# A third K-tile pair by Strassen's scheme in the FFN inputs, and sums of weights begun by an accumulating DMA

## The chip, the core and the metric

The kernel runs on one core of a Trainium2 chip. The core has a matrix engine (TensorE, PE in the profile; its weight loads are listed as PEld), a vector engine (VectorE, DVE), a scalar engine (ScalarE, ACT), a general engine (GpSimd, POOL) and a queue processor (SyncE, SP) that here only issues transfers. Each engine works through its own instruction list in order and waits at an instruction until what it needs is there. Transfers (DMAs) are issued from the lists of SP, ACT or POOL and then run on 16 shared DMA engines. The metric is the device time of one execution in microseconds (us).

## The reference

One layer of a streaming encoder on 256 tokens of width 2048, all in float32: a gated FFN, a mixer of two attentions, a cross attention to 256 memory tokens, and a second gated FFN, each followed by a residual and a layer norm. The change touches the two FFNs:

```python
D_MODEL, SEQ, D_FF = 2048, 256, 5504
def swiglu_ffn(x, w_in, w_out):
    g, u = jnp.split(x @ w_in, 2, axis=-1)
    return (jax.nn.silu(g) * u) @ w_out
...
h = layer_norm(ALPHA * h + 0.5 * swiglu_ffn(h, ffn1_w_in[l], ffn1_w_out[l]), ln_ffn1_g[l], ln_ffn1_b[l])
...
h = layer_norm(ALPHA * h + 0.5 * swiglu_ffn(h, ffn2_w_in[l], ffn2_w_out[l]), ln_ffn2_g[l], ln_ffn2_b[l])
```

All weights are read once from HBM; for each FFN `w_in` is 2048 x 11008 and `w_out` 5504 x 2048.

## The kernel before

**Numbers.** Every float32 operand is split into a rounded high part and the rest (`split`, lines 242 to 244): ScalarE casts the high part, VectorE subtracts it from the source. A product is then three passes on TensorE: high times high, low times high, high times low.

**Weights.** `run` (line 160) walks over a list of work items, each with the weights that it needs. A weight is a tile of 128 partitions by 2048 floats (1 MB), loaded by a transfer in SP's list into one of three buffers called `raw` (`fetch`, line 171). `load` (line 190) then splits it into two units of 1024 columns, each a pair of tiles `hi` and `lo`; there are four units. An item's weight is prepared at most one item ahead, since two units belong to the running item and two to the next (`ahead`, line 222). A planner arranges the instructions of each engine once, when the program is built: it takes those that are ready in an order of priority, which is the order of the code, shifted for work that is marked `SOON` or `LATE`. On the chip that order is fixed.

**FFN input.** The output columns go in groups of 512 gate and 512 up columns. A group's four results (two halves of 128 tokens, gate and up) lie in four PSUM banks, and its eight weights cover the 16 K tiles in pairs: c = 0 to 7 (`pair_group`, line 572). A plain pair is 2 K tiles x 2 token halves x 2 column halves x 3 passes, 24 matmuls of 512 columns (`mm_pair`, line 289). The groups alternate between two sets of four banks.

**Pairs by Strassen's scheme.** A pair is a product of 2 x 2 blocks (token halves by K tiles, K tiles by gate and up), and such a product can be had from seven block products instead of eight: 21 matmuls (`mm_sums`, line 322). It is done for c = 2 and c = 5 (`SUMS_IN`) in nine groups of each FFN, and for two pairs of each output group (`SUMS_OUT`). It needs three things besides:

- Sums of the activations, made once for each FFN and pair (`forms_step` and `sum_forms`, lines 302 to 320), kept in the block `X0`.
- Sums of the weight's blocks (`form_sums`, line 178). A second `raw` tile `t` takes two first sums (1024 columns, one addition of VectorE) and two further sums (512 columns each, one addition each); `t` is then split into the blocks `X2` and `X3`, of which there is one each. Two blocks of the weight itself go into units as usual. All of it stands in the code one weight ahead: `form_sums(i + 1)` is called while weight i is loaded.
- Four PSUM banks for the products that several results share. They are taken from the other set of banks at the group's first such pair, and emptied behind its last one by `shared` (line 598: two copies of ScalarE, four additions of VectorE, marked `SOON`). The next group then starts in the same banks.

The matmuls of a sum weight run in this order: six that read the first unit, three that read the second, six that read `X2`, six that read `X3`. Each group also has a tail: `hidden` (line 639) makes silu(gate) times up on ScalarE and VectorE, and transposes the result on TensorE just ahead of the next group's c = 2.

POOL's list holds transfers for the layer norms' gains and biases (`gb_apply`, line 421; `final_steps`), the attention biases and the memory tokens, and nothing in the middle of the FFN inputs.

Of the kernel before, what the change touches and what calls it, by code (L numbers as in the profile page):

```python
# [17 lines left out]
P = 128  # L18
# [6 lines left out]
F_SPLIT = (24, 19)  # L25
SUMS_IN = (2, 5)
SUMS_OUT = ((3, 8), (3, 6))
# [57 lines left out]
class Kernel:  # L85
# [74 lines left out]
    def run(self):  # L160
# [16 lines left out]

        def form_sums(i):
            raw, t = fetch(i), self.raw_tile()
            for a, b, c in ((slice(0, 1024), raw[:, 0:1024], raw[:, 512:1536]),  # L180
                            (slice(1024, 1536), t[:, 0:512], raw[:, 1024:1536]),
                            (slice(1536, 2048), t[:, 1024:1536], raw[:, 1536:2048])):
                self.nc.vector.tensor_tensor(t[:, a], b, c, ALU.add)  # L183
            sums[i] = []
            for k in range(2):
                blk = self.block(SUM_TAGS[k], (P, 2, 1024), F32R)
                self.split(t[:, k * 1024:(k + 1) * 1024], blk[:, 0, :], blk[:, 1, :])
                sums[i].append((blk[:, 0, :], blk[:, 1, :]))

        def load(i):  # L190
            w = queue[i]
            raw = fetch(i)

            for k in (i, i + 1):
                if k < len(queue) and isinstance(queue[k], Sums) and k not in sums:
                    form_sums(k)
            got = []
            if isinstance(w, Sums):
                for a, b in ((1024, 2048), (0, 512)):
                    hi, lo = self.unit()  # L200
                    self.split(raw[:, a:b], hi[:, :b - a], lo[:, :b - a])
                    got.append((hi, lo))
                return got + sums[i]
            ap, tags = w
            n = ap.shape[1]
            if tags:
                blk = [self.block(g, (P, 2048), F32R) for g in tags[:2]]
            step = 768 if ap.tensor.name.endswith("_w_in_r") else 1024
            for c in range(0, n, step):
                m = min(step, n - c)  # L210
                hi, lo = [x[:, c:c + step] for x in blk] if tags else self.unit()
                self.nc.scalar.copy(hi[:, :m], raw[:, c:c + m])  # L212

                with self.tc.issue_after(self.chain.ins) if self.chain is not None else nullcontext():
                    self.nc.vector.tensor_tensor(lo[:, :m], raw[:, c:c + m], hi[:, :m].bitcast(F32), ALU.subtract)  # L215
                got.append((hi, lo))
            return got
# [84 lines left out]
    def sum_forms(self, x, k, out):  # L302
# [6 lines left out]
        for j, (a, b, op) in enumerate(((a21, a22, ALU.subtract), (f[:, 0], a11, ALU.subtract),  # L309
                                        (a12, f[:, 1], ALU.add), (a11, a21, ALU.subtract))):  # L310
            nc.vector.tensor_tensor(f[:, j], a, b, op)
        self.split(f, out[:, 0], out[:, 1])

    def forms_step(self, e, tag, at, i, x):

        def fn():
            if i == 0:
                e["f"] = self.block(tag, (P, len(at), 2, 4, P), F32R)
            self.sum_forms(x(), 2 * at[i], e["f"][:, i])
        return fn  # L320

    def mm_sums(self, ps, qs, w, x, forms, k, first, last):
# [6 lines left out]

        n5, s2, n3, s3 = ([forms[:, a, j, :] for a in (0, 1)] for j in range(4))  # L330
        for bank, a, (hi_lo, c), own in (
# [167 lines left out]
    def ffn(self, tag, xT, st, first=None, steps=None, late=None, before=None, tags=None):  # L499
# [6 lines left out]
        for half, nf in enumerate(F_SPLIT):  # L506
            hid, fh, at = Act([]), {}, SUMS_OUT[half]
            end = half == len(F_SPLIT) - 1
            for g in range(-(-nf // 4)):
# [17 lines left out]
                if j == 0:  # L527
                    for i in range(2):
                        self.add(self.forms_step(fx, "X0", SUMS_IN, i, xT))
# [42 lines left out]
    def pair_group(self, bank, src, n, nk, x, at, fx, ps, qs, then=None):  # L572


        for c in range(-(-nk // 2)):
            kts = list(range(2 * c, min(2 * c + 2, nk)))
            ap = src[:, kts[0] * 2 * n:(kts[-1] + 1) * 2 * n]
            if c in at:
                i = at.index(c)

                def fn(w, i=i, c=c):
                    if i == 0:
                        qs.update((a, self.group_tile(bank + 1)) for a in range(4))
                    self.mm_sums(ps, qs, w, x(), fx["f"][:, i], 2 * c, i == 0, i == len(at) - 1)
                self.add(fn, Sums(ap))
# [750 lines left out]
```

## Time and profile before

| | |
|---|---|
| Median of 3 runs | 2548.22 us (2547.06 to 2551.22) |
| The profiled execution | 2548.41 us, span 2546.6 us |
| Busy, as a share of the span | PE 99%, PEld 84%, DVE 72%, ACT 50%, POOL 1% |
| Granted TensorE clock | 0.998 |
| HBM read | 482.69 MB |

The profile is taken from one execution. Each line of its list of groups gives the code line, engine, operation, the tiles written and read, the shapes and the count, then the busy time in us and the mean ns of one, then the engine's idle time just ahead and what ended it. Matmuls overlap in the engine's pipeline, so the mean of one (about 390 ns for 512 columns) is longer than the step from one to the next; the step is read from the chain of waits, which lists stretches of work with start, length and count. For a DMA the list of issues gives the size and the median time from issue to landing.

### The profile page before, as it was taken

Reading aid. Unit: us, or ns where it says so; the run is one execution under the profiler, and the core shown is the slowest. Engines: PE = TensorE matmul, PEld = TensorE weight load, DVE = VectorE, ACT = ScalarE, POOL = GpSimd, SP = SyncE. Lnnn points to the kernel's source line nnn. Section 1 sums busy time; section 2 is a strip of 40 time slices with the busy share of each in tenths; the row PEclk is TensorE's granted clock in tenths of the full one; section 3 lists DMA queues with packets and bytes.
Section 4 is the critical chain, followed back from the end, with each engine's and each line's share of the span. In section 5 each row is a group of like instructions: output and inputs, shape, how many; then the busy total and the mean of one; then the engine's idle time right before and its main releaser. Section 6 shows DMA issues by size and latency. Waiting matters only on the chain.

```text
span 2546.6 us, 32083 instructions
## 1 busy us (share of the span) xinstructions
PE 2529.7 (99%) x12620; PEld 2134.3 (84%) x12620; DVE 1824.6 (72%) x2465; ACT 1274.8 (50%) x1720; POOL 30.0 (1%) x87
## 2 busy tenths in 40 slices
PE   9999999999999999999999999999999999999998
PEld 7888888889888888888888888888888888888886
DVE  6787767786776766565657784555888877787776
ACT  5555445555454555544444564454555554455442
POOL 0000000000000000000000000000000000000000
PEclk9999999999999999999999999999999999999999
DMA  7645554555744643455556565543554555555663
GB/s 253 238 178 210 202 198 167 209 186 207 256 167 172 201 141 103 146 182 190 200 189 251 195 215 189 192 166 135 214 193 171 211 200 198 182 200 197 216 218 128
DMA packets 74038, 488.04 MB, mean 192 GB/s; under 512 B 8608, under 2 KB 8864, under 8 KB 20512
## 3 DMA queue, kind: packets, MB, share of 16 engines
q1 hardware_dynamic: 69216, 468.18, 51.7%
q0 software_dynamic: 3808, 15.73, 2.0%
q8 instruction: 98, 1.61, 0.3%
q10 hardware_dynamic: 864, 2.10, 0.2%
q14 instruction: 52, 0.43, 0.1%
HBM read 482.69 MB, written 2.10 MB: 190 GB/s over the span
## 4 chain that ended last, share of the span: by engine, by line
PE 98%; DVE 1%; DMA 1%; ACT 0%; issue 0%; DVEq 0%; ACTq 0%
PE at L296 20%; PE mm L296 19%; PE mm L284 19%; PE mm L264 17%; PE mm L265 8%; PE mm L340 5%; PE at L340 4%; PE mm L253 2%; PE at L865 1%; PE at L748 1%; PE at L895 1%; DMA raw<-ffn_w_in 1%; PE at L1165 0%; PE at L1143 0%; PE at L391 0%; PE mm L663 0%
## 5 line engine op out<-in xcount | busy, mean ns | idle before, releaser
L215 DVE TENSOR_TENSOR lo<-raw,hi 128x1024 fp32r<-128x1024 f32 (+1 forms) x752 | 904.3, 1210 | 569.2 <-ACT hi L212 559.6
L212 ACT CAST hi<-raw 128x1024 fp32r<-128x1024 f32 (+1 forms) x752 | 779.6, 1041 | 869.4 <-PE at L296 202.6
L264 PE MATMUL mm<-T,hi 128*128 128x512 f32 x1168 | 411.8, 397 | 0.0
L296 PE MATMUL mm<-hi,T 128*128 128x512 f32 (+1 forms) x1152 | 346.5, 377 | 1.5 <-ACT hi L243 1.5
L265 PE MATMUL mm<-T,lo 128*128 128x256 f32 x1168 | 326.2, 279 | 0.0
L296 PE MATMUL at<-hi,T 128*128 128x512 f32 x960 | 300.6, 389 | 0.0
L264 PEld LDWEIGHTS mm<-T,hi 128*128 128x128 f32 x1168 | 219.2, 188 | 53.5 <-issue 1.5
L296 PEld LDWEIGHTS mm<-hi,T 128*128 128x128 f32 x1152 | 214.4, 188 | 37.0 <-ACT hi L243 2.5
L264 PE MATMUL mm<-H,hi 128*128 128x512 f32 x640 | 223.3, 394 | 0.0
L265 PEld LDWEIGHTS mm<-T,lo 128*128 128x128 f32 x1168 | 220.1, 188 | 0.1
L296 PE MATMUL mm<-lo,T 128*128 128x512 f32 (+1 forms) x576 | 217.9, 378 | 0.2 <-DVE lo L244 0.2
L296 PEld LDWEIGHTS at<-hi,T 128*128 128x128 f32 x960 | 180.2, 188 | 37.2
L296 PE MATMUL at<-lo,T 128*128 128x512 f32 x480 | 187.7, 391 | 0.0
L265 PE MATMUL mm<-H,lo 128*128 128x256 f32 x640 | 177.4, 277 | 0.0
L284 PE MATMUL mm<-hi,H 128*128 128x512 f32 x568 | 176.2, 389 | 0.0
L296 PE MATMUL at<-hi,H 128*128 128x512 f32 x560 | 175.0, 389 | 0.0
L264 PEld LDWEIGHTS mm<-H,hi 128*128 128x128 f32 x640 | 120.0, 188 | 27.8
L243 ACT CAST X<-raw 128x1024 fp32r<-128x1024 f32 x96 | 100.8, 1050 | 68.6 <-DVE raw L183 68.2
L243 ACT CAST hi<-raw 128x1024 fp32r<-128x1024 f32 (+1 forms) x114 | 97.1, 855 | 66.7 <-PE at L296 31.1
L284 PE MATMUL mm<-hi,X 128*128 128x512 f32 x416 | 130.4, 391 | 0.0
L284 PEld LDWEIGHTS mm<-hi,H 128*128 128x128 f32 x568 | 106.7, 188 | 22.0
L296 PEld LDWEIGHTS at<-hi,H 128*128 128x128 f32 x560 | 105.1, 188 | 21.7
(246 smaller groups left out, 3761.9 us busy)
## 6 DMA issues: line engine op xcount, KB each, us to landing
raw<-ffn_w_in SPq DMA_DIRECT2D x151, 1024.0 KB, 4.9
raw<-ffn_w_out SPq DMA_DIRECT2D x66, 1024.0 KB, 5.0
raw<-w_gate SPq DMA_DIRECT2D x32, 1024.0 KB, 4.8
raw<-ffn_w_out_r SPq DMA_DIRECT2D x16, 1024.0 KB, 4.9
raw<-w_qk SPq DMA_DIRECT2D x16, 1024.0 KB, 4.9
raw<-w_o_b SPq DMA_DIRECT2D x16, 1024.0 KB, 4.8
raw<-w_out SPq DMA_DIRECT2D x16, 1024.0 KB, 4.8
raw<-w_xk SPq DMA_DIRECT2D x16, 1024.0 KB, 4.8
```

The lines of the kernel that those rows point to most:

```text
L212: self.nc.scalar.copy(hi[:, :m], raw[:, c:c + m])
L215: self.nc.vector.tensor_tensor(lo[:, :m], raw[:, c:c + m], hi[:, :m].bitcast(F32), ALU.subtract)
L243: self.nc.scalar.copy(hi, src)
L253: self.nc.tensor.matmul(ps, w[u][wi][:, c:c + P], x.at(xi, kt), start=(j == 0 and k == 0), stop=(j == n - 1 and k == 2),)
L264: self.nc.tensor.matmul(ps, hi, x.both(kt), start=(kt == 0), stop=False)
L265: self.last_mm = self.nc.tensor.matmul(ps[:, :S], lo, x.at(0, kt), start=False, stop=(kt == n - 1))
L284: self.last_mm = self.nc.tensor.matmul(ps, x.at(xi, kt)[:, tt * P:(tt + 1) * P], w[u][wi][:, c:c + 512], start=(start and j == 0 and k == ...
L296: self.last_mm = self.nc.tensor.matmul(ps[tt, g][:, :n], x.at(xi, kt)[:, tt * P:(tt + 1) * P], hi_lo[wi][:, g * n:(g + 1) * n], start=(kt ...
L340: self.last_mm = self.nc.tensor.matmul(bank, a[xi], hi_lo[wi][:, c:c + 512], start=own and first and j == 0, stop=own and last and j == 2)
L748: self.nc.tensor.transpose(ps[:, i * P:(i + 1) * P], s[:, c:c + P], self.ident)
L865: nc.tensor.matmul(ps[:, c0:c0 + nk], q[:, tt * P:(tt + 1) * P], k[:, :nk], start=(j == 0), stop=(j == len(parts) - 1))
L895: nc.tensor.matmul(ps[:, :S], v(0), pT[:, :S], start=True, stop=False)
```

## The change

`SUMS_IN` becomes (2, 4, 6): three of the eight pairs of each group go by Strassen's scheme. The two first sums of every sum weight, those of the FFN outputs too, are no longer added by VectorE. ScalarE copies 1024 columns of the weight into `t`, and a transfer issued from POOL adds the other 1024 columns to them in place (`accum_op=ALU.add`). These two steps (`first_sums`) stand in the code where `form_sums` stood, one weight ahead; the two further sums and the splits into `X2` and `X3` (`split_sums`) move to the sum weight's own `load`, ahead of its units. The third pair's sums of activations don't fit into `X0` and go to four small tiles of the pool `w1`, which then hold their place through the FFN.

```diff
-SUMS_IN = (2, 5)
+SUMS_IN = (2, 4, 6)
...
-        def form_sums(i):
+        def first_sums(i):
+
             raw, t = fetch(i), self.raw_tile()
-            for a, b, c in ((slice(0, 1024), raw[:, 0:1024], raw[:, 512:1536]),
-                            (slice(1024, 1536), t[:, 0:512], raw[:, 1024:1536]),
-                            (slice(1536, 2048), t[:, 1024:1536], raw[:, 1536:2048])):
-                self.nc.vector.tensor_tensor(t[:, a], b, c, ALU.add)
-            sums[i] = []
+            self.nc.scalar.copy(t[:, 0:1024], raw[:, 512:1536])
+            self.nc.gpsimd.dma_start(t[:, 0:1024], raw[:, 0:1024], accum_op=ALU.add)
+            sums[i] = t
+
+        def split_sums(i):
+            raw, t, got = fetch(i), sums[i], []
+            for a, b in ((1024, 0), (1536, 1024)):
+                self.nc.vector.tensor_tensor(t[:, a:a + 512], t[:, b:b + 512], raw[:, a:a + 512], ALU.add)
             for k in range(2):
                 blk = self.block(SUM_TAGS[k], (P, 2, 1024), F32R)
                 self.split(t[:, k * 1024:(k + 1) * 1024], blk[:, 0, :], blk[:, 1, :])
-                sums[i].append((blk[:, 0, :], blk[:, 1, :]))
+                got.append((blk[:, 0, :], blk[:, 1, :]))
+            return got
 
         def load(i):
             w = queue[i]
             raw = fetch(i)
 
-            for k in (i, i + 1):
-                if k < len(queue) and isinstance(queue[k], Sums) and k not in sums:
-                    form_sums(k)
+            if i + 1 < len(queue) and isinstance(queue[i + 1], Sums):
+                first_sums(i + 1)
             got = []
             if isinstance(w, Sums):
+                parts = split_sums(i)
                 for a, b in ((1024, 2048), (0, 512)):
                     hi, lo = self.unit()
                     self.split(raw[:, a:b], hi[:, :b - a], lo[:, :b - a])
                     got.append((hi, lo))
-                return got + sums[i]
+                return got + parts
...
-        self.split(f, out[:, 0], out[:, 1])
+        if isinstance(out, list):
+            for j in range(4):
+                self.split(f[:, j], out[j][:, 0], out[j][:, 1])
+        else:
+            self.split(f, out[:, 0], out[:, 1])
...
             if i == 0:
-                e["f"] = self.block(tag, (P, len(at), 2, 4, P), F32R)
-            self.sum_forms(x(), 2 * at[i], e["f"][:, i])
+                e["block"] = self.block(tag, (P, 2, 2, 4, P), F32R)
+            out = e["block"][:, i] if i < 2 else [self.w1((P, 2, P), F32R) for _ in range(4)]
+            self.sum_forms(x(), 2 * at[i], out)
+            e[i] = [[out[:, a, j, :] if i < 2 else out[j][:, a] for a in (0, 1)] for j in range(4)]
```

More of the change, by code (lines that the diff above doesn't have):

```diff
@@ L328, in plain @@
             return [x.at(a, kt)[:, tt * P:(tt + 1) * P] for a in (0, 1)]
-        n5, s2, n3, s3 = ([forms[:, a, j, :] for a in (0, 1)] for j in range(4))
+        n5, s2, n3, s3 = forms
         for bank, a, (hi_lo, c), own in (
@@ L527, in ffn @@
                 if j == 0:
-                    for i in range(2):
+                    for i in range(len(SUMS_IN)):
                         self.add(self.forms_step(fx, "X0", SUMS_IN, i, xT))
@@ L583, in fn @@
                         qs.update((a, self.group_tile(bank + 1)) for a in range(4))
-                    self.mm_sums(ps, qs, w, x(), fx["f"][:, i], 2 * c, i == 0, i == len(at) - 1)
+                    self.mm_sums(ps, qs, w, x(), fx[i], 2 * c, i == 0, i == len(at) - 1)
                 self.add(fn, Sums(ap))
```

## The prediction, made before the changed kernel was run

> **What bounds the kernel now.** I read the page's busy shares and its chain of waits first, to see which engine sets the end.
>
> ```profile
> span 2546.6 us, 32083 instructions
> PE 2529.7 (99%) x12620; PEld 2134.3 (84%) x12620; DVE 1824.6 (72%) x2465; ACT 1274.8 (50%) x1720; POOL 30.0 (1%) x87
> ...
> PE 98%; DVE 1%; DMA 1%; ACT 0%; issue 0%; DVEq 0%; ACTq 0%
> ```
>
> TensorE is the bound everywhere: 98% of the chain is its own work. A change gains only by fewer TensorE steps, and loses as soon as a weight is late. So I take one FFN input group and look at its chain in order of time (start us, length us, what):
>
> ```profile
> 192.59 0.55 PE at L663 x5
> 193.13 1.39 PE mm L340 x6
> 194.53 2.93 PE at L340 x12
> 197.46 0.69 PE mm L340 x3
> 198.15 10.88 PE mm L296 x48
> 209.03 1.36 PE mm L340 x6
> 210.39 2.72 PE at L340 x12
> 213.11 0.68 PE mm L340 x3
> 213.79 10.88 PE mm L296 x48
> ```
>
> L296 is a plain pair, L340 a sum pair. 48 matmuls of two plain weights take 10.88 us: 0.2267 us a step, 5.44 us a weight. The sum weight at 209.03 takes 4.76 us (to 213.79): 21 steps of 0.2267. The one at 193.13 takes 0.26 us more. Next, how busy the other engines are in this group:
>
> ```profile
> 181.30:224.70 43.40, 43.40 (x196) 35.70 (x195) 34.56 (x40) 22.72 (x27) 0.00 (x0) 1.00 0.53 194
> ```
>
> After the stretch and its length stand the busy us of PE, PEld, DVE, ACT and POOL, the clock, the DMA share and GB/s. DVE idles 8.8 of 43.4 us, ACT 20.7, the DMA engines 47%.
>
> **The change, part by part.**
>
> *Fewer matmuls.* Nine groups in each of two FFNs have a third sum pair: 18 x 3 x 0.2267 = 12.2 us less, all of it on the chain. Without any new wait the profiled execution would be 2548.4 - 12.2 = 2536.2 us. That execution is 0.2 us above the median, so I treat the two as one.
>
> *Engine work.* The groups of the window 94.5 to 268 us, shapes kept apart, and two groups of the page give the prices:
>
> ```profile
> L215 DVE TENSOR_TENSOR lo<-raw,hi 128x1024 fp32r<-128x1024 f32 x49 | 59.1, 1222 | 29.8 <-ACT hi L212 29.3
> L244 DVE TENSOR_TENSOR X<-raw,X 128x1024 fp32r<-128x1024 f32 x16 | 19.5, 1219 | 0.0
> L183 DVE TENSOR_TENSOR raw<-raw,raw 128x512 f32<-128x512 f32 x16 | 11.0, 689 | 0.3
> L183 DVE TENSOR_TENSOR raw<-raw 128x1024 f32<-128x1024 f32 x7 | 8.5, 1221 | 0.1
> L244 DVE TENSOR_TENSOR lo<-raw,hi 128x512 fp32r<-128x512 f32 x8 | 5.5, 684 | 0.0
> ```
> ```profile
> L243 ACT CAST X<-raw 128x1024 fp32r<-128x1024 f32 x96 | 100.8, 1050 | 68.6 <-DVE raw L183 68.2
> ...
> L875 POOL DMA_DIRECT2D w<-bias x16 | 8.6, 536 | 161.3 <-DVE w L881 93.4 <-DVE sm_r L741 23.8 <-PE at L748 17.2
> ```
>
> VectorE for a plain weight: 2 x 1.22 = 2.44 us. For a sum weight before: 1.22 + 2 x 0.69 + 2 x 1.22 + 1.22 + 0.68 = 6.94; after, without the first addition, 5.72. A group goes from 6 x 2.44 + 2 x 6.94 = 28.5 to 5 x 2.44 + 3 x 5.72 = 29.4 us: 0.9 more, inside 8.8 idle. ScalarE gets three copies, priced like the cast at 1.05, and the third pair's casts, together some 5 us inside 20.7. Neither becomes the bound. The third pair's activation sums (five small additions and four small splits, twice in the kernel) I cost at nothing, under the same VectorE idle time; without that cover they would be a few us in all.
>
> *The new path of a sum weight.* Before: load, then VectorE's additions and splits, a whole weight ahead. After: load, copy on ScalarE, issue on POOL, accumulating transfer, two additions, splits. Two bindings make this a loop. First, weight 4's load needs one of three `raw` buffers, and so does `t`; the buffer of weight 2 is free only when its last subtraction is done. Second, the two later additions read the weight too, so weight 4's buffer stays taken until its own accumulate has landed and been used, and only then can weight 6 be loaded. The pairs stand two apart, no longer three. SP's issues (and the subtraction that released the third) show where the buffers come free in this group:
>
> ```profile
> 186.61 0.33 SPq L175 DMA_DIRECT2D raw<-ffn_w_in  x1
> 188.88 0.33 SPq L175 DMA_DIRECT2D raw<-ffn_w_in  x1
> 190.61 0.33 SPq L175 DMA_DIRECT2D raw<-ffn_w_in  x1
> ```
> ```profile
> 188.76 1.82 DVE L244 TENSOR_TENSOR lo<-raw,hi 128x1024 fp32r<-128x1024 f32 x2
> ```
>
> The subtractions of 188.76 to 190.58 are weight 2's units: its buffer is free at 190.6. I let weight 4's load start there. Transfers cost (KB each, median us from issue to landing), and, for 1 MB loads of the group at 137 to 182 us, spread:
>
> ```profile
> raw<-ffn_w_in SPq DMA_DIRECT2D x151, 1024.0 KB, 4.9
> raw<-w_nope SPq DMA_DIRECT2D x16, 512.0 KB, 3.4
> w<-bias POOLq DMA_DIRECT2D x16, 192.0 KB, 2.6
> ```
> ```profile
> DMA to landing us min/median/max: 4.7/5.2/7.4
> ```
>
> Let Q be the time of the accumulating transfer from POOL's issue to landing. Weight 4 lands at 190.6 + 4.9 = 195.5; copied 196.6; sums landed 196.6 + Q; two additions, 198.0 + Q. Now weight 6 loads: 202.9 + Q; copied 204.0 + Q; landed 204.0 + 2Q; two additions and the low part of `X2`, 1.38 + 1.22: ready at 206.6 + 2Q. TensorE, unhindered, starts c = 2 at 193.1, c = 6 after 4.76 + 5.44 + 4.76 + 5.44 = 20.4, at 213.5, and reads `X2`'s low part after ten matmuls, at 215.8. The stall is therefore 2Q - 9.2 us a group if positive. To it comes VectorE's order: subtractions of weight 7's units that the planner puts among the additions cost 1.22 us each, none to two of them; I take one, 1.2 us, where there is a stall. For c = 4 the same sum has room until Q = 6.4: 205.6 is needed, 199.2 + Q is given. The output groups have their sum pairs three or more apart and stay unhindered by the same reckoning.
>
> *What queues behind the new waits.* On ScalarE the copy waits for a load, and casts of the plain weight between stand behind it if the planner puts them so; they are needed one weight later, 5.44 us, and take 2.1. On SP the load of weight 7 stands behind that of weight 6; it is needed at c = 7, which a stall at c = 6 pushes back as well. POOL's list holds two transfers at the end of the second FFN's inputs:
>
> ```profile
> POOL T L1193 <- PE mm L296: 556.7, 2, 548.0
> ```
>
> The second waits 8.7 us for TensorE. The accumulates of the last output group stand behind it. The first of them belongs to that group's fourth weight, three plain weights or 16 us in, so I cost this at nothing; uncovered it is 8.7 us, once.
>
> *What is Q?* The trace has no accumulating transfer. From below: the 192 KB transfer that POOL issued itself, 2.6 us; a plain 512 KB one takes 3.4. An accumulate has to read its 512 KB of target as well as its 512 KB of source, and by bytes read it is like a 1 MB load: 4.9 us alone. From above: a 1 MB load that shares the engines with another took up to 7.4. Weight 5's load is issued when weight 3's buffer comes free, near 195, so it is in flight beside the accumulate. I take 5.2, the median of loads with such overlaps in them. The stall is then 2 x 5.2 - 9.2 + 1.2 = 2.4 us, in 18 groups 43 us; less 12.2, that makes +31: 2579 us.
>
> [...]
>
> **The rivals.**
>
> *The accumulate is cheap* (faster). If Q is under 4.6 us, as a price by written bytes (3.4 us) has it, there is no stall, and the time is 2536 us (2534 to 2543). For it speaks that POOL's list is empty in the FFN inputs and that its issue takes 0.54 us; against it, the second read and weight 5's load beside it. It decides at Q = 9.2 / 2 = 4.6, where the stall begins; were VectorE's order free, the gain of 0.68 us a group would be used up at (9.2 + 0.68) / 2 = 4.9. [...]
>
> *The accumulate is very slow.* If the two reads and the collision add up to the 7.4 us of the row above, the stall is 5.6 + 1.2 = 6.8 us: 18 x 6.8 - 12.2 = +110, 2659 us. Weight 4 would be late too.
>
> *The banks come too late.* With the last sum pair at c = 6 only one plain weight, 5.44 us, lies between `shared` and the next group's start in the same banks; before, two did. The steps of `shared` are two copies and four additions in a row:
>
> ```profile
> L602 ACT COPY w<-mm 128x512 f32<-128x512 f32 x14 | 8.1, 575 | 0.0
> ...
> L606 DVE TENSOR_TENSOR w<-w,mm 128x512 f32<-128x512 f32 x14 | 9.6, 686 | 0.5
> ```
> ```profile
> DVE w L604 <- PE mm L340: 4.2, 9, 0.5
> ```
>
> 0.58 + 4 x 0.69 = 3.3 us, and in nine cases VectorE was already waiting for TensorE at L604, so the work is at the front of its queue. Some 2 us are to spare. If 3 us of other work stood ahead, it would cost 1 us a group: with a cheap accumulate 2554 us.
>
> **How the numbers follow.** Some 0.2% (5 us) is what a measurement of this kernel can tell from no change. Stall by a moderate Q (4.7 to 6.4): 0.56, 2555 to 2620 us, most likely 2579. Very slow: 0.12, above 2620. Cheap: 0.27, at 2536. Cheap with late banks: 0.05, 2543 to 2555. Faster is the cheap case, 0.27; the same 0.05; slower 0.68. The range from 2534 to 2635 us leaves out most of the very slow case, about one in ten.
>
> **What would show it.** In the profile after: 54 matmuls fewer (12566). The list of issues gets POOL's rows for the accumulate, 66 of them, whose time to landing is Q. In the list of waits TensorE, at the matmul of `mm_sums`, waits for VectorE's `X` at c = 6 of each group, for 2Q - 8 us, and not at c = 2 or c = 4. ScalarE waits for the third load, SP longer for the additions. If the group's period is 42.7 us or less, the stall is not there; if TensorE waits ahead of c = 0 for `shared`, the banks are late. The prediction is wrong if Q is under 4.6, or if the planner lets weight 6's load go ahead of the additions of weight 4.

## The result and the profile after

| | before | after |
|---|---|---|
| Median, same chip | 2547.64 us (4 runs) | 2678.44 us (2675.16 to 2680.69, 4 runs) |
| Ratio | 1 | 1.0505, 95% interval 1.0492 to 1.0518 |
| Profiled execution | 2548.41 us, span 2546.6 | 2675.16 us, span 2673.4 |
| Matmuls | 12620 | 12566 |

The change is 5% slower. The forecast was 2579 us with a range up to 2635: the sign is right, the loss is four times too small (131 us for 31). The head of the page after, and the chain of waits by engine:

```profile
span 2673.4 us, 32369 instructions
PE 2572.5 (96%) x12566; PEld 2138.9 (80%) x12566; DVE 1827.3 (68%) x2507; ACT 1355.8 (51%) x1830; POOL 86.8 (3%) x153
...
PE 51%; DMA 12%; DVE 7%; ACT 2%; issue 1%; POOL 0%; DVEq 0%; ACTq 0%; POOLq 0%; SPq 0%
```

54 matmuls are gone, as planned, and VectorE is no busier (1827.3 us for 1824.6). But TensorE fell from 98% of the chain to 51%, and transfers took 12%. No engine became the bound: the loss is waiting. TensorE's waits (line waited at, releaser: total us, times, longest; `mm` and `at` are the two sets of banks, `H` is the transposed hidden values), and the waits of SP, ScalarE and VectorE:

```profile
PE at L352 <- DVE X L249: 17.0, 24, 1.5
PE mm L352 <- DVE X L249: 17.0, 23, 1.0
PE mm L352 <- ACT X L248: 14.5, 10, 4.5
PE at L352 <- ACT X L248: 13.3, 10, 2.6
PE mm L352 <- DVE H L249: 10.3, 7, 2.5
PE at L352 <- DVE H L249: 6.5, 4, 2.1
```
```profile
SPq L175 <- DMA raw<-raw: 328.1, 60, 9.2
...
ACT X L248 <- DMA raw<-raw: 250.6, 64, 8.3
...
DVE raw L188 <- DMA raw<-raw: 171.9, 57, 6.5
```

L352 is `mm_sums` (L340 before), L175 the load, L248 and L249 the cast and subtraction in `split`, L188 the two later additions, L181 and L182 the copy and the accumulate. `raw<-raw` is the accumulating transfer. Nearly all of TensorE's waiting is at sum weights: 62 us of these rows for `X2` and `X3`, 17 for the splits of `H` at c = 2. Behind it three lists wait for the accumulate: ScalarE 250.6 us, VectorE 171.9, SP 328.1. One group of the second FFN, from the chain in order of time (start us, length us, what):

```profile
2017.04 4.47 DMA raw<-ffn_w_in
...
2022.92 4.72 DMA raw<-raw
...
2027.74 0.70 DVE raw L188
...
2028.47 0.70 DVE raw L188
...
2033.88 1.06 ACT raw L181
...
2035.22 5.92 DMA raw<-raw
...
2041.24 0.70 DVE raw L188
...
2042.58 1.22 DVE X L249
...
2047.23 7.44 DMA raw<-ffn_w_in
...
2056.09 4.51 DMA raw<-raw
```

The load of weight 6 ran just beside this chain. SP issued it right behind the second addition:

```profile
2029.23 0.33 SPq L175 DMA_DIRECT2D raw<-ffn_w_in  x1
```

It took 4.6 us and landed just ahead of the copy at 2033.88. Load, copy, accumulate, additions, next load: the loop that the prediction described is there, and it does not stop at the end of the group. The accumulate of the next group's weight 2 (2056.09) is the third in one chain. The first matmuls of c = 2, of this group and of the next, from TensorE's timeline:

```profile
2016.00 0.48 PE L352 MATMUL mm<-hi,T 128*128 128x512 f32 x1
```
```profile
2064.55 0.47 PE L352 MATMUL at<-hi,T 128*128 128x512 f32 x1
```

A period of 48.6 us, where a group took about 43.2 before.

The stalls have a second price. The windows give the clock (after the five engines' busy times):

```profile
117.60:124.40 6.80, 6.31 (x15) 4.19 (x14) 3.51 (x4) 4.50 (x6) 0.70 (x1) 0.50 0.70 243
104.00:160.00 56.00, 50.74 (x202) 39.16 (x201) 37.14 (x42) 28.52 (x34) 2.57 (x3) 0.91 0.62 199
...
2016.00:2064.60 48.60, 45.00 (x195) 36.13 (x193) 36.60 (x46) 27.41 (x33) 2.56 (x3) 0.96 0.65 206
```

From 117.6 to 124.4 us TensorE ran at half clock: 15 matmuls in 6.8 us instead of 30. The trace has 15 such stretches inside the kernel, each of 3.41 or 6.83 us and each behind a stall (the longest step between matmuls just ahead was 1.5 to 4.9 us), 64.9 us together. 136 matmuls began in them. At twice the step, 0.2267 us more for each, that is an estimate of 31 us of lost time. It is a little high: the median step inside them was 0.427 us, 0.20 more than at full clock, which makes 27.

Where the time went, by the span and the starts of the matmuls in the two traces: +126.8 us = -12.2 (matmuls) + 108 (longer steps, all inside sum weights, the half clock's part taken off) + 31 (half clock, by that estimate). Of the 108 us, 51 stand at c = 6, 38 at c = 2, 17 at c = 4, and 2 in the output groups.

### The profile page after: what moved, and what is told of

It reads as the page before. It is cut to its first block, busy times and chain, and to the rows that moved or that the text cites. A ratio compares the mean times of both kernels' runs of the same rounds, so it can differ in the third digit from the quotient of the medians.

```text
span 2673.4 us, 32369 instructions
## 1 busy us (share of the span) xinstructions
PE 2572.5 (96%) x12566; PEld 2138.9 (80%) x12566; DVE 1827.3 (68%) x2507; ACT 1355.8 (51%) x1830; POOL 86.8 (3%) x153
## 4 chain that ended last, share of the span: by engine, by line
PE 51%; DMA 12%; DVE 7%; ACT 2%; issue 1%; POOL 0%; DVEq 0%; ACTq 0%; POOLq 0%; SPq 0%
PE mm L289 16%; PE mm L269 16%; PE mm L270 8%; DMA raw<-raw 7%; DMA raw<-ffn_w_in 4%; PE mm L301 3%; PE mm L258 2%; DVE X L249 2%; PE at L301 2%; DVE lo L220 2%; DVE raw L188 1%; PE at L877 1%; DMA raw<-ffn_w_out 1%; ACT raw L181 1%; DVE lo L249 1%
## 5 line engine op out<-in xcount | busy, mean ns | idle before, releaser
L220 DVE TENSOR_TENSOR lo<-raw,hi 128x1024 fp32r<-128x1024 f32 (+1 forms) x716 | 859.3, 1209 | 441.7 <-ACT hi L217 435.7
L301 PE MATMUL mm<-hi,T 128*128 128x512 f32 (+1 forms) x1024 | 310.9, 378 | 1.1 <-ACT hi L248 0.8
L248 ACT CAST X<-raw 128x1024 fp32r<-128x1024 f32 x132 | 138.6, 1050 | 288.0 <-DMA raw<-raw 250.6
L301 PE MATMUL at<-hi,T 128*128 128x512 f32 x800 | 256.9, 394 | 0.0
L301 PEld LDWEIGHTS mm<-hi,T 128*128 128x128 f32 x1024 | 191.9, 189 | 33.0 <-ACT hi L248 1.8
L188 DVE TENSOR_TENSOR raw<-raw,raw 128x512 f32<-128x512 f32 x132 | 91.2, 691 | 176.2 <-DMA raw<-raw 171.9
L249 DVE TENSOR_TENSOR lo<-raw,hi 128x1024 fp32r<-128x1024 f32 (+1 forms) x150 | 141.6, 972 | 84.4 <-ACT hi L248 84.4
L301 PE MATMUL mm<-lo,T 128*128 128x512 f32 (+1 forms) x512 | 193.6, 378 | 0.2 <-DVE lo L249 0.2
L301 PEld LDWEIGHTS at<-hi,T 128*128 128x128 f32 x800 | 152.4, 191 | 32.8 <-ACT hi L217 0.4
L301 PE MATMUL at<-hi,H 128*128 128x512 f32 x560 | 174.9, 389 | 0.0
L249 DVE TENSOR_TENSOR X<-raw,X 128x1024 fp32r<-128x1024 f32 x132 | 160.7, 1221 | 10.5 <-ACT X L248 10.4
L301 PE MATMUL at<-lo,T 128*128 128x512 f32 x400 | 157.3, 393 | 0.3 <-DVE lo L220 0.3
L248 ACT CAST hi<-raw 128x1024 fp32r<-128x1024 f32 (+1 forms) x150 | 123.1, 845 | 23.6 <-PE mm L301 10.0
```

Of the source, the lines that this page charges most:

```text
L188: self.nc.vector.tensor_tensor(t[:, a:a + 512], t[:, b:b + 512], raw[:, a:a + 512], ALU.add)
L248: self.nc.scalar.copy(hi, src)
L249: self.nc.vector.tensor_tensor(lo, src, hi.bitcast(F32), ALU.subtract)
L301: self.last_mm = self.nc.tensor.matmul(ps[tt, g][:, :n], x.at(xi, kt)[:, tt * P:(tt + 1) * P], hi_lo[wi][:, g * n:(g + 1) * n], start=(kt ...
```

## The experiments

Each ran beside the kernel before, on the same chip. "Loss" is the median less that of before; Q is the median from POOL's issue to landing; the last column is ScalarE's total wait at the X casts for the accumulate.

| run | edit to the changed kernel | us | ratio, 95% interval | loss | Q | ACT waits |
|---|---|---|---|---|---|---|
| (after) | none | 2678.4 | 1.0492 to 1.0518 | 131 | 5.7 | 251 |
| e1 | pairs (2, 5) | 2616.1 | 1.0234 to 1.0271 | 62 | 5.0 | 174 |
| e2 | third pair, sums as before | 2548.0 | 0.9966 to 0.9992 | -6 | none | 0 |
| e3 | VectorE adds at the new place | 2546.0 | 0.9959 to 0.9985 | -8 | none | 0 |
| e16 | copy, then VectorE adds | 2549.2 | 0.9969 to 0.9993 | -5 | none | 0 |
| e4 | plain transfer, nothing added | 2616.5 | 1.0235 to 1.0274 | 63 | 4.3 | 158 |
| e5 | accumulate half | 2618.4 | 1.0233 to 1.0265 | 63 | 4.0 | 159 |
| e7 | pairs (2, 4) | 2571.3 | 1.0043 to 1.0086 | 16 | 4.7 | 144 |
| e6 | units ahead of the sums | 2690.7 | 1.0514 to 1.0552 | 135 | 5.5 | 265 |
| e10 | e1 and e6 | 2620.7 | 1.0236 to 1.0275 | 65 | 4.7 | 149 |
| e11 | additions don't read the weight | 2686.2 | 1.0514 to 1.0545 | 134 | 5.1 | 226 |
| e12 | e11, accumulate from HBM | 2720.9 | 1.0645 to 1.0700 | 171 | 5.8 | 265 |
| e8 | six idle matmuls in the stall | 2663.2 | 1.0418 to 1.0455 | 111 | 5.3 | 205 |
| e13 | one residual tile (control) | 2692.4 | 1.0514 to 1.0563 | 138 | 5.4 | 247 |
| e14 | e13, four `raw` buffers | 2710.3 | 1.0596 to 1.0645 | 156 | 5.3 | 268 |
| e18 | e14, order forced | 2674.3 | 1.0425 to 1.0487 | 120 | 6.6 | 248 |
| e19 | e18 and e6 | 2676.2 | 1.0451 to 1.0497 | 122 | 6.9 | 249 |
| e20 | e13, sums in tiles of their own | 2703.3 | 1.0584 to 1.0622 | 155 | 7.1 | 282 |
| e21 | e20, no copy on ScalarE | 2623.8 | 1.0271 to 1.0306 | 75 | 6.1 | 213 |

### Which part of the change costs

The accumulate with the old two pairs, and the third pair with the old sums:

```diff
-SUMS_IN = (2, 4, 6)
+SUMS_IN = (2, 5)
```

> The accumulating transfer alone, with the old pairs (2, 5). Loop theory: the three load buffers are held from a sum weight's load until its accumulate has landed and been used, so the weights of a whole group form one loop of about 49 us with three accumulates (load 5, copy and issue 1.35, transfer 5.7, releases); with two accumulates it is about 36 us, under TensorE's 43.2, and nothing stalls: 2544 to 2556 us, as before the change. Rival, every accumulate costs a stall of its own wherever the pairs stand (the order on ScalarE and VectorE): two thirds of the loss stay, about 2640 us.

```diff
-            self.nc.scalar.copy(t[:, 0:1024], raw[:, 512:1536])
-            self.nc.gpsimd.dma_start(t[:, 0:1024], raw[:, 0:1024], accum_op=ALU.add)
+            self.nc.vector.tensor_tensor(t[:, 0:1024], raw[:, 0:1024], raw[:, 512:1536], ALU.add)
...
-            if i + 1 < len(queue) and isinstance(queue[i + 1], Sums):
-                first_sums(i + 1)
+            for k in (i, i + 1):
+                if k < len(queue) and isinstance(queue[k], Sums) and k not in sums:
+                    first_sums(k)
+                    sums[k] = split_sums(k)
```

> The third pair alone: (2, 4, 6), but all sums on VectorE and formed one weight ahead, as before the change. Loop theory: no transfer in the loop, so the 54 matmuls come off: about 2536 us (2533 to 2546). Rival, the third pair itself is the trouble (VectorE at some 90%, one block X2 and X3 for pairs two apart): 2560 us or more.

Then only the two lines of the sum, with the new place of the rest kept; and the copy kept, with VectorE's addition in the transfer's place:

```diff
-            self.nc.scalar.copy(t[:, 0:1024], raw[:, 512:1536])
-            self.nc.gpsimd.dma_start(t[:, 0:1024], raw[:, 0:1024], accum_op=ALU.add)
+            self.nc.vector.tensor_tensor(t[:, 0:1024], raw[:, 0:1024], raw[:, 512:1536], ALU.add)
```

> The changed kernel with one edit: the first two sums by one addition of VectorE (1.22 us) in the place of ScalarE's copy and the transfer; the later sums stay in the sum weight's own load. Loop theory: each pass of the loop loses 1.35 + 5.7 - 1.3 = 5.8 us, the group's loop falls from 49 to some 32 us, TensorE is the bound again: about 2536 us (2533 to 2546). Rival, the moved stage (t and the weight held one weight longer, casts behind them) stalls by itself: above 2560 us.

```diff
-            self.nc.gpsimd.dma_start(t[:, 0:1024], raw[:, 0:1024], accum_op=ALU.add)
+            self.nc.vector.tensor_tensor(t[:, 0:1024], t[:, 0:1024], raw[:, 0:1024], ALU.add)
```

> The changed kernel with the accumulating transfer replaced by one addition of VectorE in the same place; ScalarE's copy into t stays. If the transfer's own time is the cause, and not that the sum is built in two steps by two engines, the loss is gone and the time is that of the staged addition, 2546 us, or up to 5 us more for the copies (66 x 1.05 us on ScalarE, half idle). If the copy or the hand-over from ScalarE carries a part of the loss, it stays above 2560 us.

The head of e3's page and its chain by engine:

```profile
span 2544.4 us, 32240 instructions
...
PE 2524.8 (99%) x12566; PEld 2128.8 (84%) x12566; DVE 1894.2 (74%) x2573; ACT 1299.4 (51%) x1764; POOL 29.8 (1%) x87
...
PE 92%; DVE 5%; DMA 2%; ACT 1%; issue 1%; ACTq 0%; DVEq 0%; SPq 0%
```

The transfer is the cause, alone. Without it the third pair is a small gain in all three forms (ratios 0.9972, 0.9979, 0.9981), whether the later steps stand early or late and whether the sum is made in one step or in two on two engines. It costs VectorE 67 us of work (1894.2 for 1827.3), which its idle time holds. And e3 beats both kernels, by 0.28% (0.15 to 0.41) against the one before. With the transfer, even two pairs, three and five weights apart, lose 62 us: that was to be nearly free by the prediction's reckoning, and neither forecast of e1 (2544 to 2556, or about 2640) fits it.

### Is it the adding, or the trip?

```diff
-            self.nc.gpsimd.dma_start(t[:, 0:1024], raw[:, 0:1024], accum_op=ALU.add)
+            self.nc.gpsimd.dma_start(t[:, 0:1024], raw[:, 0:1024])
```

> The changed kernel with a plain transfer from POOL in the place of the accumulating one (it overwrites instead of adding, so the sums are not formed): same bytes written, same places, waits and order. If the second read is what makes it long, time to landing falls from 5.7 to about 3.7 us and the loop theory gives 3 x 2 us less a group: 2678 - 18 x 6 = about 2570 us. If the collision with the weight loads is what makes it long, it stays above 5 us and the time above 2640 us.

```diff
-            self.nc.gpsimd.dma_start(t[:, 0:1024], raw[:, 0:1024], accum_op=ALU.add)
+            self.nc.gpsimd.dma_start(t[:, 0:512], raw[:, 0:512], accum_op=ALU.add)
+            self.nc.vector.tensor_tensor(t[:, 512:1024], t[:, 512:1024], raw[:, 512:1024], ALU.add)
```

> The changed kernel with half the accumulate: 512 columns by the transfer, the other 512 by an addition of VectorE (0.69 us). With a plain transfer, time to landing fell from 5.7 to 4.3 us and the kernel by 62 us, 2.5 us a group for each us of the transfer, near the 3 of the loop theory. Half the bytes should land in about 4.3 us too, less 0.7 us of VectorE's addition in the loop: 2620 to 2645 us. If the number of transfers counts and not their length, about 2678 us.

(The plain transfer leaves the first sums unformed.) The issue rows of after, of e4 and of e5:

```profile
raw<-raw POOLq DMA_DIRECT2D x66, 512.0 KB, 5.7
```
```profile
raw<-raw POOLq DMA_DIRECT2D x66, 512.0 KB, 4.3
```
```profile
raw<-raw POOLq DMA_DIRECT2D x66, 256.0 KB, 4.0
```

By the medians adding costs 1.4 us of 5.7; the other 4.3 are the trip. Whether the 1.4 us are a read of the target, as the prediction reckons, no run shows by itself. Half the bytes still take 4.0 us: a smaller accumulate halves the loss, and 63 us of it stay. Between Q = 4.3 and 5.7 the loss goes from 63 to 131 us: some 49 us for each us of Q, where the prediction's 18 stalls of 2Q give 36. By an estimate about 20 of these 68 us are the clock (64.9 us at half clock for 23.9 in e4, counted half; the granted clocks were 0.986 and 0.994); the rest is 34 us for each us of Q. So the slope was right. The level was not: at e4's Q the formula has no stall at all (2 x 4.3 is under 9.2), and 63 us are lost.

### The clock

Six matmuls that add zero are put ahead of the first one that reads `X2`, in all 54 input sum weights. That is 324 x 0.2267 = 73 us of work.

```diff
+            if c == 0 and hi_lo is t13:
+                for _ in range(fill):
+                    self.nc.tensor.matmul(ps[0, 1], self.mask[:, P:2 * P].bitcast(F32R), u1[0][:, 0:512], start=False, stop=False)
```

> The changed kernel with six matmuls by a block of zeros ahead of the first matmul that reads X2, in the 54 sum pairs of the FFN inputs (they add nothing to the results): 54 x 6 x 0.2267 = 73 us of TensorE work, put where it mostly stalls, so that the clock is not halved. In the changed kernel the clock stood at half for 65 us apart from the end, at most 32 us lost. If the clock's loss comes on top of the stalls, half-clock time falls under 20 us and the time to 2640 to 2665 us. If the loop of loads and accumulates sets the group's time, the time moves by less than 15 us either way. If the fill is not hidden, it rises by up to 73 us.

73 us more work, and the kernel is 20 us faster against its own before (loss 111 for 131). The half-clock stretches fell from 64.9 to 6.8 us (granted clock 0.986 and 0.997), which accounts for an estimated 29 us, half of the difference; by that all but some 9 us of the zero matmuls ran in time that was a stall. So the clock's part of the loss is real, and follows from the stalls.

### Which way does the wait travel?

The runs that follow try the loop through the three `raw` buffers, and the order of the work. Two pairs two apart:

```diff
-SUMS_IN = (2, 4, 6)
+SUMS_IN = (2, 4)
```

> Two pairs two apart, (2, 4), with the accumulating transfer; as many matmuls as before the change. With (2, 5) it was 2616 us. If what costs is the order of the work at c = 2, about the same: 2605 to 2630 us. If each step of two costs by itself, the stall at c = 4 comes on top: above 2640 us. If the loop round the whole group with three accumulates were all, no stall: 2550 us, which (2, 5) already speaks against.

The loop inside a group would make this worse than (2, 5); it is far better, 16 us for 62, and none of the three forecasts has it. What grows from (2, 4, 6) to (2, 5) to (2, 4) is the room from a group's last sum weight to the next group's first: 4, 5 and 6 weights, with losses of 131, 62 and 16. That fits a chain which recovers in that stretch, or doesn't; the prediction took the stretch as free. It is not shown by itself, since the first kernel has three accumulates a group for two, and the other two differ in both distances.

The units first (in three and two pairs):

```diff
-                parts = split_sums(i)
                 for a, b in ((1024, 2048), (0, 512)):
...
-                return got + parts
+                return got + split_sums(i)
```

> The changed kernel with one order turned round: in a sum weight's load, the splits of its two units stand ahead of the later sums and of X2 and X3. Loop theory: after c = 2 the load of weight 4 is freed right after the additions instead of some 2.5 us later, the loop falls from 49.3 to about 47 us: about 2640 us, with TensorE still stalled at c = 6. Order theory (TensorE waits because splits that it needs are queued behind work that waits for the accumulate): more than half of the loss goes, below 2610 us.

> Pairs (2, 5) with the accumulating transfer, and the units' splits ahead of the sums. In the run with (2, 5) TensorE waited 26 us for the units' low parts and 15 us for the transposed hidden values, both queued on VectorE behind additions that wait for the accumulate. Order theory: the first wait goes, and part of the clock's loss: 2570 to 2595 us. Loop theory alone: no change, 2610 us or more.

In the three pairs (e6) nothing is won, against both forecasts. In e1 TensorE waited for the units' low parts (18.0 + 7.6 us). In e10 that is 1.0 us, but it waits for the hidden values' `H` instead, 24.1 + 18.0 us for 8.0 + 7.2, and the loss is the same. Next, the weight's buffer is let go earlier: ScalarE copies the other half of the weight too, so the additions read only `t`; and in the second run the accumulate's source is HBM.

```diff
+            self.nc.scalar.copy(t[:, 1024:2048], raw[:, 1024:2048])
...
-                self.nc.vector.tensor_tensor(t[:, a:a + 512], t[:, b:b + 512], raw[:, a:a + 512], ALU.add)
+                self.nc.vector.tensor_tensor(t[:, a:a + 512], t[:, b:b + 512], t[:, a:a + 512], ALU.add)
```

> The changed kernel with the weight's buffer set free by its own splits: ScalarE copies the other 1024 columns of the weight into t as well (1.05 us more), and the later additions read t alone, so no buffer waits for the accumulate except t. In the changed kernel SP waited 328 us, 60 times, for an accumulate. If that hold is what makes the group a loop, weight 6 and the next group's first weight are loaded some 3 to 5 us earlier and the group falls from 48.5 to about 44 or 45 us: 2585 to 2625 us. If only the transfer's own length counts (VectorE's work behind its landing), the time stays within 15 us of 2678, or rises with ScalarE's copies.

```diff
-            self.nc.gpsimd.dma_start(t[:, 0:1024], raw[:, 0:1024], accum_op=ALU.add)
+            self.nc.gpsimd.dma_start(t[:, 0:1024], queue[i].ap[:, 0:1024], accum_op=ALU.add)
```

> As the run with the buffer set free, and the transfer adds the 1024 columns straight from HBM instead of from the weight's buffer. In that run SP still waited 314 us for accumulates, since the transfer itself reads the buffer; here nothing but the weight's own splits and copies holds it. Loop theory: weight 6 and the next group's first weight are loaded 4 to 6 us earlier, the groups fall from 49 to 50 us to about 44 to 46 us: 2580 to 2625 us, SP's wait for accumulates mostly gone. If the transfer's length and VectorE's work behind it set the time whatever the buffer does: 2660 us or more.

No gain: in e11 the transfer itself reads the buffer, and SP still waits for it (314.4 us); in e12 SP's wait for accumulates is about half as long (132.0 and 35.5 us for transfers from the two FFN weights, loads among them), and the kernel is slower, with 5.8 us for the accumulate and 34.6 MB more from HBM. Then a fourth buffer, made room for by one residual tile for both token halves, with that alone as control:

```diff
-        self.h = [self.res.tile([P, D], F32, tag=f"h{i}", name=f"h{i}") for i in range(2)]
+        self.h = [self.res.tile([P, D], F32, tag="h0", name="h0")] * 2
```

> Control for the next run: the changed kernel with one residual tile h for both token halves (the halves overwrite each other, so the output is not the reference's; the work is the same). It only frees 8 KB of memory per partition. All theories: the FFN inputs take as long as in the changed kernel, about 2678 us; the outputs' and norms' steps on h may wait for each other, up to some 15 us more.

```diff
-        self.wraw = pool("wraw", 3)
+        self.wraw = pool("wraw", 4)
```

> As the control, with the 8 KB used for a fourth buffer for weights and sums (same output, not the reference's). Loop theory (three buffers, of which a sum weight and its t hold two until the accumulate has landed and been split, so that the next loads wait): weight 6 and the next group's weights are loaded ahead, the groups fall from about 49 us to TensorE's 42.5 to 44, and most of the loss goes: 2540 to 2585 us above or below with the control's offset taken off. If the transfer's length and the place of its work in the engines' order set the time, at least half of the loss stays: 2615 us or more.

Slower than its control, by 18 us. The timelines of e14's VectorE and ScalarE show what the planner did with it (in brackets the idle time before, and its releaser):

```profile
2077.98 1.28 DVE L249 TENSOR_TENSOR H<-mm,H 128x512 fp32r<-128x512 f32 x2
2085.70 0.69 DVE L188 TENSOR_TENSOR raw<-raw,raw 128x512 f32<-128x512 f32 x1 [6.44 <-issue]
2086.31 1.22 DVE L249 TENSOR_TENSOR lo<-raw,hi 128x1024 fp32r<-128x1024 f32 x1
```
```profile
2077.66 1.58 ACT L248 CAST hi<-raw 128x1024 fp32r<-128x1024 f32 x2
2085.70 1.05 ACT L248 CAST X<-raw 128x1024 fp32r<-128x1024 f32 x1 [6.46 <-DMA raw<-raw]
2088.22 1.05 ACT L248 CAST X<-raw 128x1024 fp32r<-128x1024 f32 x1 [1.47 <-DVE raw L188]
2089.95 1.06 ACT L181 COPY raw<-raw 128x1024 f32<-128x1024 f32 x1 [0.68 <-DVE lo L249]
```

The unit's subtraction at 2086.31 was ready when its cast ended near 2079; it stood 6.4 us behind an addition that waited for the transfer. And the next sum weight's copy (2089.95), with which its accumulate begins, stands behind casts that wait for this one's, and then waits for a subtraction of this weight too. So the order was forced, without and with the units first:

```diff
-                parts = split_sums(i)
+                with self.tc.issue_after(self.last_hi.ins), self.tc.issue_after(self.last_lo.ins):
+                    parts = split_sums(i)
...
-                self.nc.scalar.copy(hi[:, :m], raw[:, c:c + m])
+                self.last_hi = self.nc.scalar.copy(hi[:, :m], raw[:, c:c + m])
```

> Four raw buffers (one residual tile for both token halves, so the output is not the reference's), and the later additions, the X casts and the X subtractions of a sum weight are put behind the last cast and the last subtraction of the plain weight ahead of it. With four buffers alone the planner had put the additions, which wait for the accumulate, ahead of subtractions that were ready. Theory A (three buffers make the loop, and the fourth did not help only because ready work stood behind a wait): most of the loss goes, 2545 to 2640 us. Theory B (the sums of one weight follow those of the one before on ScalarE's and VectorE's lists, the copy of the next behind the X casts of the last, so that each accumulate is in the chain whatever the buffers): 2670 us or more.

> The kernel with four buffers and the order put right, and besides the two units of a sum weight are cast and subtracted ahead of its sums. Under theory A the units no longer wait behind the additions: as fast as without that or a few us faster, below 2640. Under theory B no gain: 2670 or more, with TensorE waiting for X instead of for the units' low parts.

Both come out as theory B has it (2674 and 2676 us). The order is worth some 36 us against e14; order and buffer together are worth 18 against the control, and no run has the order forced with three buffers. It was not yet a clean test of the buffers: with four buffers `t` falls on the buffer of the sum weight before, so the copy still waits for the earlier sums. In the last two runs the sums get two tiles of their own and the further sums are added in place; then the copy is taken from ScalarE as well, by loading those columns a second time (0.5 MB more for each sum weight).

```diff
-            raw, t = fetch(i), self.raw_tile()
+            raw, t = fetch(i), self.wsum.tile([P, 1024], F32, tag="sum", name=self.name("sum"))
...
-            for a, b in ((1024, 0), (1536, 1024)):
-                self.nc.vector.tensor_tensor(t[:, a:a + 512], t[:, b:b + 512], raw[:, a:a + 512], ALU.add)
+            for a, src in ((1024, t[:, 0:512]), (1536, raw[:, 1024:1536])):
+                self.nc.vector.tensor_tensor(raw[:, a:a + 512], src, raw[:, a:a + 512], ALU.add)
```

> The first sums get two tiles of their own (1024 columns), the further sums are added in place in the weight's tile, the units are split ahead of them, and the order behind the plain weight's splits stays forced (one residual tile for both token halves makes the room, so the output is not the reference's). Weight 6's load and its sum tile no longer wait for weight 4's additions; but its copy still stands on ScalarE's list behind the cast of weight 4's X2, which waits for weight 4's accumulate. If the buffers were the loop: 2535 to 2570 us. If the chain runs through ScalarE's list as well: between 2580 and 2670, with ScalarE waiting 150 us or more for the accumulates.

```diff
-            self.nc.scalar.copy(t[:, 0:1024], raw[:, 512:1536])
+            self.nc.sync.dma_start(t[:, 0:1024], queue[i].ap[:, 512:1536])
```

> The kernel with sum tiles of their own, and the copy of ScalarE replaced by a load of the same 1024 columns straight into the sum tile (0.5 MB more from HBM for each of 66 sum weights). Now no step that makes weight 6's sums waits for weight 4's: if the loss came from that chain, whichever way it ran, it goes: 2535 to 2570 us, though each accumulate takes 5 us or more. If it stays above 2600 us, the accumulate's traffic itself holds up the loads, and the chain is not the cause.

ScalarE's waits in e20, and below them ScalarE's and TensorE's in e21 (`mm_sums` is L353 there, the copy of e20 L182, the split L249 and L250):

```profile
ACT X L249 <- DMA sum<-raw: 281.7, 61, 9.2
...
ACT sum L182 <- DMA raw<-ffn_w_in: 70.3, 20, 5.2
```
```profile
ACT X L249 <- DMA sum<-raw: 212.6, 49, 12.4
```
```profile
PE mm L353 <- DVE H L250: 21.2, 9, 3.3
PE at L353 <- DVE H L250: 11.4, 6, 4.0
PE at L353 <- DVE X L250: 5.5, 9, 0.8
```

With the buffers out of the chain and the copy still in ScalarE's list (e20) the loss is 155 us, more than its control's 138 and above both forecasts. With the copy out of ScalarE's list as well it is 75, though 34.6 MB more are read. So the theory of the buffers alone falls. In the changed kernel itself ScalarE sat idle ahead of 59 of its 66 copies, waiting for a load or for VectorE:

```profile
ACT raw L181 <- DMA raw<-ffn_w_in: 72.2, 31, 3.8
ACT raw L181 <- DVE lo L220: 28.8, 19, 2.2
```

In e20 it was idle ahead of only 26, each time for a load; the other 40 followed without a pause on work in its list, 28 of them on a stretch of work that began with an `X` cast which had waited for VectorE's additions. So once the buffers are out of the way, the copy in ScalarE's in-order list carries the chain from one accumulate to the next, and taking it out removes half of the loss. How much of these 80 us is the order of the list stays open: e21 also saves the copy's own 1.05 us, up to 57 us for 54 weights. Neither forecast for e21 (2535 to 2570, or above 2600 with the chain no cause) fits: what e21 takes out of the chain is about half of the loss. The largest wait left in e21 is for `H`, at c = 2: 32.6 us of TensorE's waits, against 12.3 for anything of `X` in the three sums together. VectorE's and ScalarE's lists around it:

```profile
2071.56 1.23 DVE L250 TENSOR_TENSOR lo<-raw,hi 128x1024 fp32r<-128x1024 f32 x1 [2.72 <-ACT hi L249]
...
2079.26 1.28 DVE L250 TENSOR_TENSOR H<-at,H 128x512 fp32r<-128x512 f32 x2
```
```profile
2069.52 1.05 ACT L249 CAST X<-sum 128x1024 fp32r<-128x1024 f32 x1 [2.95 <-DMA sum<-raw]
...
2077.80 1.06 ACT L249 CAST H<-at 128x512 fp32r<-128x512 f32 x2
```

The hidden values' splits stand behind the `X` work of weight 2, which began when its accumulate landed. How much of the last 75 us is this order, and how much the transfers' own traffic (weight loads take 6.1 us in the median in e21 and 4.8 in e16), no run tells apart. It stays open.

## Why the prediction was wrong, point by point

**What bounds, and the gain.** Right in the matmuls, and about half in the time. 54 matmuls are fewer, and where the transfer is absent 5 to 8 us of the 12.2 arrive. In e3 4.5 us of TensorE's waits are for `H`, where the kernel before has 0.8; where the others went was not shown.

**Engine work.** Right. VectorE's load, ScalarE's copies and the third pair's activation sums cost nothing that e2, e3 or e16 shows. The banks of `shared` were no trouble either: no matmul of a plain pair (L301) is in the list of TensorE's waits with more than a microsecond. Ten of the twelve sum weights of the output groups ran their 4.76 us. POOL's issue took 0.86 us, not 0.54.

**Q.** Taken as 5.2, measured 5.7 in the median. By the prediction's own formula that makes 2 x 5.7 - 9.2 + 1.2 = 3.4 us a group, 2597 us: a small part of the miss.

**The loop's length.** Right, and closely. From weight 4's load to `X2`'s low part for weight 6 the formula gives 16.0 + 2Q; with this group's 4.72 and 5.92 us that is 26.6. The chain shows 2017.04 to 2043.80: 26.8.

**Where the loop starts.** This is the step that failed: "its buffer is free at 190.6. I let weight 4's load start there", 2.5 us ahead of c = 2's start at 193.13. After, the load starts at 2017.04, 1.0 us behind c = 2's start at 2016.00. Weight 2's own sums come from an accumulate as well, and everything that follows it in the lists is late with it. The prediction put the time into the two later sum weights and gave weight 2 its old times. With these it took the stretch from c = 6 to the next c = 2 as free. The chain instead runs through all three accumulates of a group and on into the next one, so a group never catches up: its period is 48.6 us, against 43.2 - 0.7 + 2.4 = 44.9 forecast. At c = 6, where the forecast had 43 us of stalls, 51 stand. That this is so near is partly luck: in e4, where the formula has none, 39 us stand at c = 6.

**"Not at c = 2 or c = 4."** Wrong for the same reason: the stalls stand at all three sums, 38 us at c = 2 (partly as waits for `H`) and 17 at c = 4, both put at nothing.

**What queues behind the waits.** Too cheap. The prediction looked at the copy's wait for a load, and not at ScalarE's casts and VectorE's additions that wait for the accumulate: 250.6 and 171.9 us at the heads of in-order lists. e21 against e20 shows that the copy of the next sum weight, which stands behind those casts, is worth some 80 us with its own time, once the buffers are free.

**The clock.** Not in the sum at all: an estimated 31 us. The granted clock was 0.998 before, and the sum took every step at 0.2267 us.

The 96 us between the forecast and the profiled execution are 38 at c = 2, 17 at c = 4, 8 at c = 6 (51 for 43), 2 in the output groups, and 31 of the clock.

**The rivals.** The cheap accumulate was out by Q, 5.7 for 4.6 at most; and e4 shows that a Q under 4.6 would not have saved it. "Very slow" forecast 2659 us, near the result, but from Q = 7.4: right size, wrong mechanism. The late banks didn't show.

## What to carry to other kernels

When a step of an engine becomes a transfer, its time moves into a chain, and the question is what must be finished before the next such transfer can start: buffers, but just as much every in-order list in which the next one's first step stands behind a wait for this one. Reckon the first instance of a repeating pattern with the delay in it, and follow the chain once round the period: a stretch with slack in the old trace has none if the new chain passes through it. Where TensorE is the bound, price a stall with the clock that it loses (here 64.9 us at half clock, some 30 us lost).

## What the runs showed of the hardware

- In the trace after, half clock came in stretches of 3.41 us (eleven) and 6.83 us (four), besides the end of the kernel. Their starts lie whole multiples of 3.413 us apart, over 2.4 ms. The median step between matmuls was 0.427 us inside them, 0.227 at full clock. One of the 15 followed 3.41 us without a matmul start, behind the longest step between matmuls, 4.85 us. In the 3.41 us ahead of the other 14, 1 to 6 matmuls started, where 15 start at full pace (3.41 / 0.2267), and four of these stretches followed steps of no more than 1.53 us. Counted in stretches of 3.413 us from these starts, the trace has 760 at full clock: the 13 with up to five starts were all followed by half clock (once by that of the end), three of five with six, and none of 742 with seven or more. That is one trace; what sets the clock it does not show.
- Medians of a transfer from POOL, beside the weight loads: within the core's memory 4.3 us plain for 512 KB (e4), 5.7 accumulating (after; 4.7 in e7 and e10, 7.1 in e20), 4.0 accumulating 256 KB (e5); 5.8 accumulating 512 KB from HBM (e12, FFN inputs). The accumulate's issue held POOL for 0.86 us (median, after).
- With more freedom to start loads the loads took longer. From three buffers (e13) to four (e14) the loads of the FFN inputs went from 4.8 to 5.9 us, the accumulate from 5.4 to 5.3; with four and the order forced (e18) they took 6.1 and 6.6 us. Whether they slow each other down is not shown by itself.
